# MLP of a two-layer trunk: down groups run in turns with up tiles, with seven products instead of eight for 5 of 8 pairs

## The chip, the cores and the metric

The kernel runs on one core of one Trainium2 chip. The core has five engines that run side by side, each through its own queue of instructions in a fixed order: TensorE (PE: matmuls out of SBUF into PSUM), VectorE (DVE) and ScalarE (ACT) for elementwise work, GpSimd (POOL) for elementwise work that touches SBUF alone, and SyncE (SP), which issues the loads here. Engines wait for each other by semaphores. The metric is the device time of one execution in microseconds (us); the runs of one kernel are given by their median.

## The reference

The trunk has two layers over 256 tokens of 2048 features (float32). Each layer is an attention part (a banded one in the first layer, a stick-breaking one in the second, both beside a memory attention), an output projection, and a squared-ReLU MLP. The change concerns the MLP:

```python
def rms_norm(x, g):
    xf = x.astype(jnp.float32)
    y = xf * lax.rsqrt(jnp.mean(xf * xf, axis=-1, keepdims=True) + EPS)
    return (y * g.astype(jnp.float32)).astype(x.dtype)

def sq_relu_mlp(h, g, w_in, w_out):
    return jnp.square(jax.nn.relu(rms_norm(h, g) @ w_in)) @ w_out
    # h (256, 2048), w_in (2048, 8192), w_out (8192, 2048)
```

Both products are wanted at close to float32 precision.

## The kernel before, in words

**Precision.** Every weight and every activation is split in two: `hi` is the value rounded to the fast matmul type (fp32r), `lo` is what is left of it. A product is then three matmuls, hi·hi, hi·lo and lo·hi. ScalarE makes `hi` (a cast, L173, L227, L249), VectorE makes `lo` (a subtraction, L176, L228, L250). Nearly all of VectorE's work is this.

**Weights.** They come as a stream of units of 128x1024 floats, in the order in which TensorE uses them. `weights()` hands out the next unit and keeps three more prepared ahead (`AHEAD = 3`); preparing one is the load, the cast and the subtraction. The pools hold 6 raw units, 4 `hi` and 5 `lo`, so no engine can run further ahead of TensorE than that.

**The MLP** goes through the 8192 hidden features in four chunks of 2048 (c = 0 to 3), 16 tiles of 128 features each. An *up tile* (f = 0 to 15) multiplies the normed input by 16 blocks of w_in: 16 matmuls 512 wide with `hi` weights (against both halves of the activation at once) and 16 matmuls 256 wide with `lo` weights. Its sum leaves PSUM by a copy on ScalarE (`low`) and an addition on VectorE. The norm's factor, which is one number per token, is applied behind the product: before the change `up` squares relu(x) on VectorE (L1138), and `finish` multiplies by the reciprocal of the mean square (`r_mlp`, made once in a layer by `inverse_square`: one matmul `inv`, L552, and a reciprocal on VectorE, L553) on VectorE (L1093), casts on ScalarE (L1094), and subtracts on GpSimd (L1095). Up tiles run in twos (`two_tiles`).

**Down groups.** After the 16 up tiles of a chunk come its down groups. A group is 1024 output features; two groups of four (g = 0 and 1 together, g = 2 and 3 together) make one `pair_group`, n = 0 or 1, which runs over the chunk's eight pairs j of feature tiles (2j, 2j+1). For one pair there are two ways. *Direct*: two units of weights, each 4 products, 8 in all, 24 matmuls 512 wide. *Sevenfold*: the 2x2 block form with seven products (Winograd's form of Strassen's), 21 matmuls 512 wide in four units of weights; its weight sums are made on VectorE (L222 to L226), and its sums of activations too (L1111), with their splits (L1124, L1125). The table `SEVEN` says which pairs are sevenfold: 25 in the first layer and 26 in the second, of 56 in each. A group's eight accumulators take all eight banks of PSUM, so up tiles and groups cannot be mixed. In the last chunk the second half of the outputs is done plainly (`tokens_major`, and by features at the very end).

**Order.** TensorE's instructions stand in program order. Those of the other engines are put in an order by a scheduler when the program is built, and stay in it.

## Time and profile before

| what | value |
|---|---|
| time, median of 3 runs | 2166.73 us (2166.26 to 2167.32) |
| span of the profiled execution | 2165.4 us, 1.3 us under that median |
| TensorE busy | 2158.2 us (100%) |
| VectorE busy | 1690.1 us (78%) |
| ScalarE busy | 1191.3 us (55%) |
| GpSimd busy | 326.7 us (15%) |
| read from HBM | 410.58 MB, 191 GB/s |
| first MLP | from about 440 us to 1130 us |
| second MLP | from about 1475 us to the end |

The span runs from the first to the last instruction of one execution. Busy is the time in which an engine had an instruction under way. Matmuls overlap: the recorded duration of one (389 ns for 512 columns) is longer than the distance at which the next one starts, and the distance is what counts.

### The profile page before, as it was taken

To read this page: it belongs to the slowest core of one execution; us is meant where nothing else is said; L and a number is where in the kernel's file an instruction comes from. 1 tells how busy PE (TensorE), PEld (TensorE's weight loads), DVE (VectorE), ACT (ScalarE), POOL (GpSimd) and SP (SyncE) were. 2 spreads that over 40 slices of the span, in tenths; PEclk is the share of its full clock that TensorE was granted. 3 is DMA by queue.
4 is the path that set the end of the run, shared out by engine and by line. 5 is a ranking of instruction groups with operands and counts; after the bars stand their busy time and mean duration, and the time that the engine had idled before them with its cause. 6 is when DMAs were issued, how large, how long until landed. Compare 5 with 4: busy or idle time off the path is not lost.

```text
span 2165.4 us, 30280 instructions
## 1 busy us (share of the span) xinstructions
PE 2158.2 (100%) x11083; PEld 1852.1 (86%) x11083; DVE 1690.1 (78%) x2431; ACT 1191.3 (55%) x1668; POOL 326.7 (15%) x349
## 2 busy tenths in 40 slices
PE   9999999999999999999999999999999999999999
PEld 8888888888888888888888889888888888988887
DVE  7778885678977987997886556567797798799796
ACT  7744545555655555555555447655565556555553
POOL 0010112621001001001050112352100100100100
PEclk9999999999999999999999999999999999999999
DMA  9655556655765765666666654455676577667665
GB/s 325 197 165 185 168 179 195 198 192 166 212 205 178 208 213 178 194 219 189 202 180 191 185 190 136 131 188 183 182 201 224 164 203 223 188 180 219 190 180 156
DMA packets 213317, 414.66 MB, mean 191 GB/s; under 512 B 13232, under 2 KB 144304, under 8 KB 213168
## 3 DMA queue, kind: packets, MB, share of 16 engines
q1 hardware_dynamic: 212592, 410.63, 62.0%
q8 instruction: 87, 1.43, 0.3%
q10 hardware_dynamic: 576, 2.10, 0.3%
q14 instruction: 62, 0.51, 0.1%
HBM read 410.58 MB, written 2.10 MB: 191 GB/s over the span
## 4 chain that ended last, share of the span: by engine, by line
PE 98%; DVE 1%; DMA 0%; issue 0%; ACT 0%; SPq 0%
PE acc L77 94%; PE yp L77 1%; PE accs L77 1%; PE tp L77 1%; PE s L77 1%; PE z L77 1%; DMA raw<-in_w_mem 0%; DVE lo L176 0%; DVE pt L640 0%; DVE lo L250 0%; DVE h L998 0%; ACT hi L173 0%; DVE kvx L465 0%; ACT hi L249 0%; PE stat L77 0%
## 5 line engine op out<-in xcount | busy, mean ns | idle before, releaser
L176 DVE TENSOR_TENSOR lo<-raw,hi 128x1024 fp32r<-128x1024 f32 (+1 forms) x524 | 642.6, 1237 | 308.4 <-ACT hi L173 183.3
L173 ACT CAST hi<-raw 128x1024 fp32r<-128x1024 f32 (+1 forms) x524 | 546.4, 1045 | 375.8 <-PE acc L77 316.7
L77 PE MATMUL acc<-hi,hid 128*128 128x512 f32 x1474 | 481.4, 389 | 0.0
L77 PE MATMUL acc<-mlpx,hi 128*128 128x512 f32 x2048 | 472.6, 390 | 0.0
L77 PEld LDWEIGHTS acc<-mlpx,hi 128*128 128x128 f32 x2048 | 382.0, 188 | 77.7
L77 PEld LDWEIGHTS acc<-hi,hid 128*128 128x128 f32 x1474 | 276.7, 188 | 57.5
L77 PE MATMUL acc<-lo,hid 128*128 128x512 f32 x737 | 286.7, 389 | 0.0
L1095 POOL TENSOR_TENSOR hid<-upsq,hid 128x256 fp32r<-128x256 f32 x128 | 122.3, 964 | 1086.2 <-ACT hid L1094 1086.2
L227 ACT CAST hi<-raw 128x1024 fp32r<-128x1024 f32 x204 | 192.1, 946 | 132.8 <-PE acc L77 56.0
L77 PEld LDWEIGHTS acc<-mlpx,lo 128*128 128x128 f32 x2048 | 250.6, 192 | 2.8
L77 PE MATMUL acc<-mlpx,lo 128*128 128x256 f32 x2048 | 252.0, 283 | 0.0
L228 DVE TENSOR_TENSOR lo<-raw,hi 128x1024 fp32r<-128x1024 f32 x204 | 222.8, 1108 | 29.6 <-ACT hi L227 28.0
L249 ACT CAST hi<-raw 128x1024 fp32r<-128x1024 f32 x146 | 154.0, 1055 | 126.1 <-PE acc L77 104.5
L77 PE MATMUL acc<-hi,xg 128*128 128x512 f32 x640 | 208.4, 398 | 0.0
L250 DVE TENSOR_TENSOR lo<-raw,hi 128x1024 fp32r<-128x1024 f32 x146 | 179.2, 1228 | 14.4 <-ACT hi L249 13.7
L77 PEld LDWEIGHTS acc<-lo,hid 128*128 128x128 f32 x737 | 138.4, 188 | 28.5
L77 PEld LDWEIGHTS acc<-hi,xg 128*128 128x128 f32 x640 | 120.2, 188 | 24.6
L451 ACT COPY low<-acc 128x256 f32<-128x256 f32 x188 | 69.1, 368 | 112.2 <-PE acc L77 111.9
L77 PE MATMUL acc<-lo,xg 128*128 128x512 f32 x320 | 124.7, 390 | 0.7 <-DVE lo L176 0.7
L77 PE MATMUL acc<-y,hi 128*128 128x512 f32 x512 | 119.9, 391 | 0.0
L77 PEld LDWEIGHTS acc<-y,hi 128*128 128x128 f32 x512 | 95.0, 188 | 19.0
L1094 ACT CAST hid<-upsq 128x256 fp32r<-128x256 f32 x128 | 51.9, 407 | 75.6 <-DVE upsq L1093 75.4
(202 smaller groups left out, 2610.4 us busy)
## 6 DMA issues: line engine op xcount, KB each, us to landing
raw<-in_w_up SPq DMA_DIRECT2D x256, 512.0 KB, 4.4
raw<-in_w_down SPq DMA_DIRECT2D x256, 512.0 KB, 5.6
raw<-in_w_in SPq DMA_DIRECT2D x80, 512.0 KB, 3.7
raw<-in_w_o SPq DMA_DIRECT2D x64, 512.0 KB, 4.0
raw<-in_w_mem SPq DMA_DIRECT2D x28, 512.0 KB, 5.9
raw<-in_w_kv_v SPq DMA_DIRECT2D x24, 512.0 KB, 3.9
raw<-in_w_kv_k SPq DMA_DIRECT2D x24, 512.0 KB, 4.2
raw<-in_w_q SPq DMA_DIRECT2D x24, 512.0 KB, 4.1
```

What stands on the lines that cost most here:

```text
L77: return self._tc.keep_in_program_order(fn(*args, **kwargs))
L173: nc.scalar.copy(hi[:, :n], raw[:, :n])
L176: nc.vector.tensor_tensor(lo, raw, hi.bitcast(F32), op=ALU.subtract)
L227: nc.scalar.copy(hi4, src)
L228: nc.vector.tensor_tensor(lo4, src, hi4.bitcast(F32), op=ALU.subtract)
L249: nc.scalar.copy(hi4, turned)
L250: nc.vector.tensor_tensor(lo4, turned, hi4.bitcast(F32), op=ALU.subtract)
L451: nc.scalar.copy(low[:], bank[:, T:])
L1094: nc.scalar.copy(hid[:, f, :T], a[:])
L1095: nc.gpsimd.tensor_tensor(hid[:, f, T:], a[:], hid[:, f, :T].bitcast(F32), op=ALU.subtract)
```

## The change

The change reorders the MLP and raises the number of sevenfold pairs.

- `SEVEN = [5, 5]`: in each of the 14 group pairs (seven in a layer), pairs j = 0 to 4 are sevenfold and j = 5 to 7 direct. That is 70 sevenfold pairs, where there were 51.
- `weave` gives each group eight up tiles to run in turns with: n = 0 gets the own chunk's tiles 8 to 15, n = 1 the next chunk's tiles 0 to 7. A group starts with one up tile, one sevenfold pair, one up tile, and so on (with direct units between them where n = 1). The activations of a layer live in one `hid` tile, whose features are overwritten as the group before them is through with them. The first chunk of each layer starts with its tiles 0 to 7 in `halves_first` and `two_tiles`, as before.
- PSUM: the accumulator "22" shares two banks with "p1" and "p5", which leaves a fourth bank in the pool that up tiles use.
- `inverse_square` is replaced by `inverse_root`: the mean square (VectorE, L576) is raised to the power -0.5 by a GpSimd instruction on 128x256 elements (L577). The factor `ri` is now applied ahead of the square: `finish` does max(x, 0) * ri on VectorE (L1168) and the square on ScalarE (L1171). The subtraction of the split moves from GpSimd to VectorE (`split`, L1126 and L1127).
- `block_sums` makes the sums of activations of a sevenfold pair (L1149 to L1152), one set for both groups.

Core of the diff:

```diff
-SEVEN = [
-    [(FOUR, FOUR), (THREE, FOUR), (THREE, FOUR), (THREE,)],
-    [(FOUR, FOUR), (THREE, FOUR), (THREE, FOUR), (FOUR,)],
-]
+SEVEN = [5, 5]
+BY_TURNS = 8
...
-    def inverse_square(acc, name):
+    def inverse_root(acc, name):
 
         ps = ps_y.tile([P, 512], F32, name="inv", tag="y")
         mm(ps[:, :T], neg_ones[:], acc[:], True, True)
-        r2 = const.tile([P, T], F32, name=f"r2_{name}", tag="r2")
-        nc.vector.tensor_scalar(r2[:], ps[:, :T], -1.0 / D, EPS, op0=ALU.mult, op1=ALU.add)
-        nc.vector.reciprocal(r2[:], r2[:])
-        return r2
+        ri = const.tile([P, T], F32, name=f"ri_{name}", tag="ri")
+        nc.vector.tensor_scalar(ri[:], ps[:, :T], -1.0 / D, EPS, op0=ALU.mult, op1=ALU.add)
+        nc.gpsimd.tensor_tensor(
+            ri[:], ri[:], neg_half[:, 0:1].to_broadcast([P, T]), op=ALU.pow
+        )
+        return ri
...
+        def split(hi, lo, src):
+            nc.scalar.copy(hi, src)
+            nc.vector.tensor_tensor(lo, src, hi.bitcast(F32), op=ALU.subtract)
+
+        def block_sums(c, j, a, b):
...
+            nc.vector.tensor_tensor(s23[:, P:], a11, a21, op=ALU.subtract)
+            nc.vector.tensor_tensor(s1, a21, a22, op=ALU.add)
+            nc.vector.tensor_tensor(s23[:, :P], s1, a11, op=ALU.subtract)
+            nc.vector.tensor_tensor(s14[:, P:], a12, s23[:, :P], op=ALU.subtract)
+            for home in homes[1:] if whole else homes:
+                split(*home)
...
-            def finish(f, hid=hid, squares=squares, factors=factors, c=c):
-                a = squares[f]
-                nc.vector.tensor_tensor(a[:], a[:], inv["r2"][:], op=ALU.mult)
-                nc.scalar.copy(hid[:, f, :T], a[:])
-                nc.gpsimd.tensor_tensor(
-                    hid[:, f, T:], a[:], hid[:, f, :T].bitcast(F32), op=ALU.subtract
+        def finish(c, f):
+            squares, factors = chunks[c]
+            a = squares[f]
+            nc.vector.scalar_tensor_tensor(
+                out=a[:], in0=a[:], scalar=0.0, in1=inv["ri"][:], op0=ALU.max, op1=ALU.mult
+            )
+            nc.scalar.activation(a[:], a[:], AF.Square)
+            if f // 2 >= sevens:
+                split(hid[:, f, :T], hid[:, f, T:], a[:])
+            elif f % 2 == 1:
+                split(hid[:, f, :T], hid[:, f, T:], a[:])
+                factors[f // 2] = block_sums(c, f // 2, squares.pop(f - 1), a)
...
+        for c, n, kind, i in mlp_steps(l):
+            if kind == "H":
+                halves_first(xg_, FIRST_UP, lambda f, b: up(0, f, b))
+                continue
+            if kind == "T":
+                two_tiles(xg_, [lambda b, f=f: up(0, f, b) for f in (i, i + 1)])
+                continue
+            if kind == "U":
+                features_major(xg_, lambda b, c=c, i=i: up(c, i, b))
+                continue
```

Three places in the order of the built programs matter below.

GpSimd at the start of the first layer's MLP, before (`sq` and `mlpsq` are the sums of squares that the norm needs, `upsq` a squared up tile, `kvsq` belongs to what follows the MLP):

```order
L963 TENSOR_TENSOR low_4145<-low,h_3211 128x256
L483 TENSOR_TENSOR sq<-h_3211 128x256
L484 TENSOR_TENSOR mlpsq_3214<-mlpsq_3214,sq 128x256
L1095 TENSOR_TENSOR hid_0_4160<-upsq,hid_0_4160 128x256 x16
L1095 TENSOR_TENSOR hid_1_5756<-upsq,hid_1_5756 128x256 x16
```

and with the change:

```order
L988 TENSOR_TENSOR low_4145<-low,h_3211 128x256
L507 TENSOR_TENSOR sq<-h_3211 128x256
L508 TENSOR_TENSOR mlpsq_3214<-mlpsq_3214,sq 128x256
L577 TENSOR_TENSOR ri_mlp_4279<-ri_mlp_4279,neg_half 128x256
L504 TENSOR_TENSOR kvsq<-h_3205 128x256
```

The subtractions of a layer (16 for each of four chunks) are gone from GpSimd, and one power instruction has come.

VectorE in the same place, before (`inv` is the sum over features in PSUM):

```order
L552 TENSOR_SCALAR r_mlp_4283<-inv 128x256
L553 RECIPROCAL r_mlp_4283<-r_mlp_4283 128x256
L1093 TENSOR_TENSOR upsq<-upsq,r_mlp_4283 128x256 x2
L176 TENSOR_TENSOR lo_4312<-raw_4310,hi_4311 128x1024
L176 TENSOR_TENSOR lo_4326<-raw_4324,hi_4325 128x1024
L1132 TENSOR_TENSOR up<-acc,low 128x256
```

and with the change, from 20 rows behind L576 on, at the end of the weights of the first sevenfold pair:

```order
L250 TENSOR_TENSOR raw_0_4596<-raw_0_4596 128x4x128
L252 TENSOR_TENSOR lo_4678<-raw_1_4598,hi_4677 128x1024
L252 TENSOR_TENSOR lo_4684<-raw_0_4596,hi_4683 128x1024
L1168 SCALAR_TENSOR_TENSOR up<-up,ri_mlp_4279 128x256 x6
L1149 TENSOR_TENSOR s_4466<-up 128x128
L1127 TENSOR_TENSOR hid_4160<-up,hid_4160 128x256
L1150 TENSOR_TENSOR up<-up 128x128
L1151 TENSOR_TENSOR s_4466<-up 128x128
L1127 TENSOR_TENSOR hid_4160<-up,hid_4160 128x256
```

The first use of the norm's factor stood directly behind its making; now it stands behind the last weights that can be prepared ahead, and all later weights stand behind it.

TensorE, with the change, from the end of up tile 8 into the first sevenfold pair of the first group (`mlpx` is the MLP's input, `hid` its activations, `s_x` and `s_w` sums of activations):

```order
L101 MATMUL acc<-mlpx_3213,lo_4546 128x256 x8
L101 MATMUL acc<-mlpx_3213,lo_4560 128x256 x8
L101 MATMUL acc<-hi_4600,hid_4160 128x512
L101 MATMUL acc<-lo_4601,hid_4160 128x512
L101 MATMUL acc<-hi_4600,hid_4160 128x512 x2
L101 MATMUL acc<-lo_4601,hid_4160 128x512
L101 MATMUL acc<-hi_4600,hid_4160 128x512
L101 MATMUL acc<-hi_4612,s_x 128x512
```

where before the other up tiles of the chunk stood (here tiles 8 and 9):

```order
L77 MATMUL acc<-mlpx_3213,lo_4555 128x256 x8
L77 MATMUL acc<-mlpx_3213,lo_4569 128x256 x8
L77 MATMUL acc<-mlpx_3213,lo_4595 128x256 x8
L77 MATMUL acc<-mlpx_3213,lo_4609 128x256 x8
L77 MATMUL acc<-mlpx_3213,lo_4658 128x256 x8
```

The first matmul that reads finished activations has moved forward by seven up tiles.

399 lines of the change are left out of this document (208 added, 191 removed).

## The prediction

> **What bounds the kernel now.** I read the page first, then the chain of waits, then a table of stretches, then the instructions around the start of an MLP.
>
> ```profile
> span 2165.4 us, 30280 instructions
> PE 2158.2 (100%) x11083; PEld 1852.1 (86%) x11083; DVE 1690.1 (78%) x2431; ACT 1191.3 (55%) x1668; POOL 326.7 (15%) x349
> PE 98%; DVE 1%; DMA 0%; issue 0%; ACT 0%; SPq 0%
> 449.37 643.53 PE acc L77 x3297
> 1484.29 521.83 PE acc L77 x2670
> 449.00:777.00 328.00, 328.00 (x1666) 281.11 (x1665) 276.11 (x373) 187.57 (x249) 30.18 (x32) 1.00 0.65 194
> 777.00:1093.00 316.00, 316.00 (x1637) 272.09 (x1636) 263.50 (x360) 170.10 (x225) 30.86 (x32) 1.00 0.65 199
> sum 1290.00, PE 1290.00 PEld 1107.92 DVE 1087.83 ACT 721.22 POOL 122.25; mean PE 322.50 PEld 276.98 DVE 271.96 ACT 180.31 POOL 30.56
> ```
>
> Line 3 is the share of each engine in the chain that ended last; lines 4 and 5 are two of its pieces (start, length, what). TensorE is never left waiting for 644 us in the first MLP and 522 us in the second. The table of stretches (width, then busy time of PE, PEld, DVE, ACT, POOL; its sum is over the two MLPs, 1290 us) has TensorE busy in all of it and VectorE in 1087.83 of 1290 us, 84%. So a matmul less is time less, as long as VectorE, which makes every `lo`, keeps ahead.
>
> The price of a matmul is the distance to the next one:
>
> ```profile
> 451.11 14.70 PE L77 MATMUL acc<-mlpx,hi 128*128 128x512 f32 x64
> 465.64 7.83 PE L77 MATMUL acc<-mlpx,lo 128*128 128x256 f32 x64
> 473.31 14.70 PE L77 MATMUL acc<-mlpx,hi 128*128 128x512 f32 x64
> ```
>
> 64 matmuls of 512 columns take 465.64 - 451.11 = 14.53 us, 0.227 each; 64 of 256 columns take 7.67 us, 0.120 each. An up tile (16 and 16) is 5.55 us, a sevenfold pair (21 wide) 4.77 us, a direct unit (12 wide) 2.72 us.
>
> **The change part by part.** *Products.* 70 - 51 = 19 pairs go from 8 products to 7, each product 3 matmuls: 57 wide matmuls less, 57 x 0.227 = **12.9 us less**. Switching between wide and narrow matmuls costs nothing visible at 465.64 and 473.31, so the new order costs TensorE nothing of its own.
>
> *VectorE in the mixed groups.* Its price is again the distance between starts:
>
> ```profile
> 530.26 0.41 DVE L1138 SCALAR_TENSOR_TENSOR upsq<-up 128x256 f32<-128x256 f32 x1
> 530.60 1.21 DVE L228 TENSOR_TENSOR lo<-raw,hi 128x1024 fp32r<-128x1024 f32 x1
> 531.73 0.42 DVE L1093 TENSOR_TENSOR upsq<-upsq,r_mlp 128x256 f32<-128x256 f32 x1
> 543.54 0.69 DVE L222 TENSOR_TENSOR raw<-raw 128x512 f32<-128x512 f32 x1
> 544.27 0.69 DVE L223 TENSOR_TENSOR raw<-raw,raw 128x512 f32<-128x512 f32 x1
> 546.48 0.68 DVE L225 TENSOR_TENSOR raw<-raw,raw 128x512 f32<-128x512 f32 x1
> 547.08 1.22 DVE L228 TENSOR_TENSOR lo<-raw,hi 128x1024 fp32r<-128x1024 f32 x1
> L1111 DVE TENSOR_TENSOR s<-upsq x62: 277/720/823, 472.5 to 2066.1; 128x128 f32<-128x128 f32 x62
> L1111 DVE TENSOR_TENSOR s<-s,upsq x31: 277/279/283, 474.3 to 2066.8; 128x128 f32<-128x128 f32 x31
> ```
>
> A 256-wide operation holds VectorE 0.34 us, a 1024-wide 1.13, a 512-wide 0.60 (0.73 when the next needs its result; 0.65 on average), a 128-wide 0.28. The first L1111 form has a median of 720 ns where 277 is possible; it is the one that starts while GpSimd subtracts (L1095), and the change takes those subtractions off GpSimd, so I count 0.28. Up tile: 2 x 1.13 + 3 x 0.34 = 3.28 (the subtraction that moves here replaces the multiplication that is merged away). Sevenfold pair: 4 x 0.65 + 3 x 1.13 + 0.60 = 6.6. Sums for one pair, beyond the splits counted: 4 x 0.28 + 0.34 + 0.28 = 1.74. A whole n = 1 group with its eight up tiles: 8 x 3.28 + 5 x 6.6 + 6 x 1.13 + 4 x 1.74 + 9 evacuations at 0.60 = 78.4 us, against 8 x 5.55 + 5 x 4.77 + 6 x 2.72 = 84.6 us of TensorE: 93%. An n = 0 group makes sums for one pair: 73.2 against 84.6. On the whole VectorE fits. Inside a group it is tight: two turns without a direct unit (tiles 3 and 4 of an n = 1 group) are 2 x 9.88 + 1.74 = 21.5 us against 20.6, so 0.9 us is lost in each of the six n = 1 groups if nothing is prepared ahead (5.4 us), nothing if the usual three units are. I take **2 us**. ScalarE gets 128 squares and has room (721 of 1290 us busy).
>
> *The power on GpSimd.* This is the term that decides. The factor was made by a reciprocal on VectorE at 449.86 and used at 451.65:
>
> ```profile
> 448.93 0.43 PE inv L77 x2
> 449.40 0.42 DVE L552 TENSOR_SCALAR r_mlp<-inv 128x256 f32<-128x256 f32 x1 [0.20 <-PE inv L77]
> 449.86 1.75 DVE L553 RECIPROCAL r_mlp<-r_mlp 128x256 f32<-128x256 f32 x1
> 451.65 0.76 DVE L1093 TENSOR_TENSOR upsq<-upsq,r_mlp 128x256 f32<-128x256 f32 x2
> ```
>
> Now GpSimd raises 256 columns to the power -0.5. No row shows that size. The nearest:
>
> ```profile
> L571 POOL TENSOR_TENSOR sroot<-msq,neg_half x20: 1007/1012/1983, 59.5 to 1221.1; 128x4 f32<-128x4 f32 x20
> L483 POOL TENSOR_TENSOR sq<-h x45: 610/796/1592, 366.8 to 1475.3; 128x256 f32<-128x256 f32 x45
> L720 POOL TENSOR_SCALAR_AFFINE_SELECT sp<-sp x12: 407/408/409, 1298.1 to 1384.2; 128x256 f32<-128x256 f32 x12
> L155 POOL TENSOR_SCALAR_AFFINE_SELECT neg_tri<-neg_ones 128x128 f32<-128x128 f32 x1 | 0.3, 293 | 0.0
> ```
>
> (minimum/median/maximum ns in the first three.) The same power takes 1007 ns for only **4** columns, where a multiplication of 256 takes 610: the power is dear by the column. How much of the 1007 is fixed? The select takes 293 ns for 128 columns and 408 for 256, so 0.9 ns a column and 178 fixed. A multiplication reads two operands and cannot be cheaper by the column, so at most 610 - 256 x 0.9 = 380 ns of it is fixed. Then the power costs between (1007 - 380)/4 = 157 and (1007 - 178)/4 = 207 ns a column, and 256 columns **40.6 to 53.2 us**. I take 42, near the end that comes from the same kind of instruction. (Were the 1007 ns all fixed, it would be about 1 us: the first rival.)
>
> What hides it: TensorE's work from 449.4 to the first use of finished activations. In the new order that is the rest of tiles 2 and 3, tiles 4 to 7 and tile 8: 112 wide and 96 narrow matmuls in all. That is to 473.31 by the rows above, then 32 wide (7.26) and tile 8 (5.55): 486.1 us. The power starts at about 449.9 and ends at 491.9. Behind it VectorE has six scalings, then the splits and sums in its order; up to the split of feature tile 0 that is 12 operations of 256 and 8 of 128, 12 x 0.34 + 8 x 0.28 = 6.3 us, and the first matmul needs only ScalarE's half of that split, some 0.5 us sooner: 5.8. So the first sevenfold pair starts at 497.7 and not at 486.1: **11.6 us lost**.
>
> Then VectorE is late, because everything queued behind the first scaling waited with it: all later weights, the evacuations of tiles 6 to 8, the splits of eight tiles, the sums of four pairs. From the end of the power to the last `lo` of the third sevenfold pair its order holds 10 of 1024 (11.3), 2 of 512 (1.2), 8 weight sums (5.2), 31 of 256 (10.5) and 25 of 128 (7.0): 35.2 us. TensorE needs that unit 3 x 4.77 + 2 x 5.55 - 1.36 = 24.0 us behind its restart, so at 5.8 + 24.0 = 29.8: **5.4 us more** (0 if ScalarE and VectorE overlap better than I add up). Further on a turn is 9.88 of VectorE against 10.3 of TensorE, so the lag does not grow. ScalarE's squares stand behind the same wait, with the casts of later weights behind them; they are the shorter queue.
>
> Per layer 11.6 + 5.4 = 17.0; two layers **34.0 us**. Sum: -12.9 + 34.0 + 2 = +23.1 on a span of 2165.4: 2188.5, and with the 1.3 us by which the median lies over it, 2189.8. I say **2190**.
>
> The Trainium skill speaks of the power's engine: "GPSIMD Engine Reference", section "Performance versus the Vector engine", has about 2.6 cycles per element for ordinary elementwise work there (4497 ns for an addition of 2048 columns). By that rule 256 columns would be an estimated 0.6 us (an eighth of it), which agrees with the row of 610 ns for a multiplication and not with 1007 ns for 4 columns of a power; by it the power would be hidden and the sum be -12.9 + 2.
>
> **The rivals.** *A, the power is cheap* (its 1007 ns are a fixed cost). It hides whenever it takes under 486.1 - 5.8 - 449.9 = 30.4 us; the whole change breaks even where a layer's loss is about 6 us, near 31 us. For it: no row shows that the cost grows with columns. Against it: 1007 ns is 2.5 times the largest fixed cost that the other GpSimd rows allow (380). Time: 2166.7 - 12.9 = 2154, **faster**.
> *B, the power at its upper end*, 53.2 us: 11.2 more in each layer, 2190 + 22 = 2212. For it: the fixed cost of the one operation measured at two sizes (178 ns).
> *C, VectorE becomes the bound in all mixed groups*: if operations cost their recorded duration (1.22 for 1024, 0.42 for 256) because each waits for ScalarE's cast, a turn is 3.7 + 7.1 = 10.8 us against 10.3; five turns in 14 groups, 70 x 0.5 = 35 us on top: 2225. For it: 93% load and only three units ahead. Against it: TensorE did not wait at all in the old groups, which held four sevenfold pairs with two direct units each (6.6 + 2 x 1.13 = 8.9 of VectorE against 10.2).
> *D, the lag is milder*: the wait is there, but nothing is lost behind it and in the groups: 2166.7 - 12.9 + 2 x 11.6 = 2177, and 2174 with the power at 40.6.
>
> **How the numbers follow.** Forecast (2180 to 2200) 0.55, D 0.13, B 0.14, C 0.07, A 0.08, something else 0.03. A measurement of this kernel tells about 0.2% (4.3 us) from no change. Only A is faster; a power of 30 to 33 us would end within 0.2%, which I give 0.03. So faster 0.08, same 0.03, slower 0.89. The range leaves out A, most of C and the end of B: 2172 to 2214.
>
> **What would show it.** Right: one GpSimd instruction L577 of some 42 us at the start of each MLP; a hole in TensorE of about 12 us behind up tile 8, near 486 and as far behind `inv` in the second layer, with L1168 released by L577 in the waits of VectorE; short holes in the second and third sevenfold pairs; no holes from the fifth pair on; 57 matmuls fewer; L1149 to L1152 near 0.28 us. Wrong: L577 of a few us (then A), holes in every turn (then C), or holes at the tiles that share one PSUM bank, 13 to 15 of a chunk, of which I expect none, since a direct unit of 2.72 us stands between them, in which VectorE's part of the evacuation is 0.34 us.

## The result: 2227 us, slower by more than predicted

| kernel | median of its runs | ratio to the kernel before, 95% interval |
|---|---|---|
| before | 2166.75 us (2166.26 to 2167.32) | |
| with the change | 2227.16 us (2225.93 to 2228.55) | 1.0279 (1.0265 to 1.0294) |

The change makes the kernel 60 us slower. I had predicted 2190, with 2214 as the upper end: the direction is right, the size is not. The page of the changed kernel, its parts 1 and 4:

```profile
span 2225.6 us, 30260 instructions
PE 2168.3 (97%) x11026; PEld 1842.7 (83%) x11026; DVE 1745.2 (78%) x2597; ACT 1246.7 (56%) x1828; POOL 285.5 (13%) x223
PE 87%; DVE 6%; POOL 4%; ACT 1%; issue 1%; DMA 0%; SPq 0%; ACTq 0%; DVEq 0%
```

TensorE has 57 matmuls less (11083 before), as the change says. Without waits this would be a span of 2165.4 - 12.9 = 2152.5 us; the span is 2225.6, so 73 us are lost. The chain of waits was 98% TensorE before and is 87% now, with GpSimd in it for the first time. The groups of instructions tell what TensorE's MLP matmuls waited for (busy time, mean ns of one, then idle time ahead of them and what ended it; before the change all these matmuls had 0.0, as in the first row here, which is of the kernel before), and the row of the power stands below them:

```profile
L77 PE MATMUL acc<-mlpx,hi 128*128 128x512 f32 x2048 | 472.6, 390 | 0.0
```

```profile
L101 PE MATMUL acc<-mlpx,hi 128*128 128x512 f32 x2048 | 490.5, 393 | 8.9 <-DVE up L1186 8.9
L101 PE MATMUL acc<-hi,hid 128*128 128x512 f32 x1404 | 476.3, 392 | 20.1 <-ACT hid L1126 20.1
L101 PE MATMUL acc<-lo,hid 128*128 128x512 f32 x702 | 276.5, 394 | 7.9 <-DVE lo L252 7.9
L101 PE MATMUL acc<-hi,s_w 128*128 128x512 f32 x280 | 99.5, 393 | 1.5 <-ACT hi L251 1.5
L101 PE MATMUL acc<-lo,s_w 128*128 128x512 f32 x140 | 56.8, 406 | 6.9 <-DVE lo L252 6.8
L101 PE MATMUL acc<-lo,s_x 128*128 128x512 f32 x80 | 31.7, 396 | 3.8 <-DVE lo L252 3.8
L577 POOL TENSOR_TENSOR ri_mlp<-ri_mlp,neg_half 128x256 f32<-128x256 f32 x2 | 82.3, 41140 | 14.3 <-DVE ri_mlp L576 14.3
```

That is 20.1 us for finished activations (the two holes behind the power), 8.9 us for an up tile's PSUM bank, and 20.1 us in four rows for the weights' `hi` and `lo`. Together 49.1 us. (The sum is smaller than 73, since a wait counts as idle only once the recorded 0.39 us of the matmul ahead are over, 0.16 us more than its distance to the next, and since part of the loss is a slower clock, 8.8 us, and some 9 us lie in distances that are a little longer, each by too little to count as idle.)

**The start of an MLP.** The chain of waits there, in order of time (start, length, what):

```profile
449.60 41.15 POOL ri_mlp L577
...
490.77 2.10 DVE up L1168 x6
...
505.96 0.34 DVE up L1186
...
506.44 13.73 PE acc L101 x54
```

and TensorE's own timeline (the bracket is the idle time ahead and what ended it):

```profile
483.92 2.07 PE L101 MATMUL acc<-mlpx,lo 128*128 128x256 f32 x16
496.06 0.80 PE L101 MATMUL acc<-hi,hid 128*128 128x512 f32 x1 [10.07 <-ACT hid L1126]
496.66 0.63 PE L101 MATMUL acc<-lo,hid 128*128 128x512 f32 x1
497.08 1.05 PE L101 MATMUL acc<-hi,hid 128*128 128x512 f32 x2
...
506.44 6.76 PE L101 MATMUL acc<-mlpx,hi 128*128 128x512 f32 x16 [3.98 <-DVE up L1186]
```

```profile
485.00:497.00 12.00, 1.93 (x11) 1.58 (x10) 8.34 (x24) 5.73 (x17) 5.74 (x1) 0.65 0.28 88
497.00:535.00 38.00, 33.32 (x144) 27.14 (x143) 33.35 (x62) 21.40 (x39) 0.00 (x0) 0.88 0.43 126
```

The power takes 41.15 us; the first sevenfold pair starts at 496.06 behind a hole of 10.07. Then a second hole: up tile 9 needs a bank whose evacuation (L1186, at 505.96) stands in VectorE's queue behind the splits of eight tiles. Behind each hole the granted clock is low (0.65 and 0.88 on the mean in the two stretches, the number ahead of the DMA share): 0.42 us from one wide matmul to the next instead of 0.23, and 6.76 us for 16 of them where 3.79 is usual. The Trainium skill, "TensorE: Matmul & The Clock Gate", section "Part 1: The HAM clock gate", says that the clock is halved behind an idle window of about 3.4 us and comes back after as long of work; the holes of 10.07 and 3.98 us agree. The clock is back after 2.9 and 6.1 us of matmuls (at 498.93 and 512.58). Run e1, below, has half clock behind a hole of only 1.94 us, which that sentence would not lead one to expect.

**The later groups.** (A turn, in what follows, is one up tile and one sevenfold pair, 10.3 us of TensorE.) One wait of a pattern that comes back in every layer and chunk, on the chain of waits around 871 us (third sevenfold pair of an n = 0 group):

```profile
871.39 0.38 ACT low L475
...
871.80 0.42 DVE up L1186
872.23 0.60 DVE raw L249
872.82 0.34 DVE up L1168
873.16 0.96 DVE lo L252
...
874.21 0.69 DVE raw L250
...
874.93 1.06 ACT hi L251
...
876.01 1.24 DVE lo L252
```

TensorE waits for `lo` at 874.1, for `hi` at 876 and for `lo` again at 877.2. The weight sums (L249, L250) and the subtractions of this pair come late in VectorE's queue. Measured by the distances of the matmuls' starts, such waits sum to some 15 us in each layer, mostly 2.3 to 3.4 us in an n = 0 group and 1.1 to 1.3 in an n = 1 group.

### The profile page after: what moved, and what is told of

Same layout as the page of the kernel before. It is cut to its first block, busy times and chain, and to the rows that moved or that the text cites. A ratio compares the mean times of both kernels' runs of the same rounds, so it can differ in the third digit from the quotient of the medians.

```text
span 2225.6 us, 30260 instructions
## 1 busy us (share of the span) xinstructions
PE 2168.3 (97%) x11026; PEld 1842.7 (83%) x11026; DVE 1745.2 (78%) x2597; ACT 1246.7 (56%) x1828; POOL 285.5 (13%) x223
## 4 chain that ended last, share of the span: by engine, by line
PE 87%; DVE 6%; POOL 4%; ACT 1%; issue 1%; DMA 0%; SPq 0%; ACTq 0%; DVEq 0%
PE acc L101 83%; POOL ri_mlp L577 4%; DVE lo L252 2%; PE yp L101 1%; PE accs L101 1%; PE tp L101 1%; PE s L101 1%; PE z L101 1%; ACT hi L251 0%; DVE raw L250 0%; DVE up L1168 0%; ACT hi L197 0%; DVE raw L249 0%; DVE up L1186 0%; DVE hid L1127 0%
## 5 line engine op out<-in xcount | busy, mean ns | idle before, releaser
L200 DVE TENSOR_TENSOR lo<-raw,hi 128x1024 fp32r<-128x1024 f32 (+1 forms) x524 | 640.3, 1236 | 243.1 <-ACT hi L197 211.1
L197 ACT CAST hi<-raw 128x1024 fp32r<-128x1024 f32 (+1 forms) x524 | 540.9, 1044 | 357.4 <-PE acc L101 293.1
L101 PE MATMUL acc<-mlpx,hi 128*128 128x512 f32 x2048 | 490.5, 393 | 8.9 <-DVE up L1186 8.9
L101 PE MATMUL acc<-hi,hid 128*128 128x512 f32 x1404 | 476.3, 392 | 20.1 <-ACT hid L1126 20.1
L251 ACT CAST hi<-raw 128x1024 fp32r<-128x1024 f32 (+1 forms) x280 | 263.8, 944 | 221.1 <-DVE raw L247 147.6
L252 DVE TENSOR_TENSOR lo<-raw,hi 128x1024 fp32r<-128x1024 f32 (+1 forms) x280 | 302.3, 1086 | 41.1 <-ACT hi L251 36.4
L101 PEld LDWEIGHTS acc<-hi,hid 128*128 128x128 f32 x1404 | 265.0, 189 | 73.3 <-ACT hid L1126 20.6
L101 PE MATMUL acc<-lo,hid 128*128 128x512 f32 x702 | 276.5, 394 | 7.9 <-DVE lo L252 7.9
L101 PEld LDWEIGHTS acc<-mlpx,lo 128*128 128x128 f32 x2048 | 261.1, 191 | 9.5 <-DVE lo L200 0.3
L101 PE MATMUL acc<-mlpx,lo 128*128 128x256 f32 x2048 | 265.0, 283 | 0.0
L274 DVE TENSOR_TENSOR lo<-raw,hi 128x1024 fp32r<-128x1024 f32 x108 | 133.2, 1233 | 46.6 <-ACT hi L273 46.5
L273 ACT CAST hi<-raw 128x1024 fp32r<-128x1024 f32 x108 | 113.9, 1054 | 84.7 <-PE acc L101 65.6
L101 PE MATMUL acc<-hi,s_w 128*128 128x512 f32 x280 | 99.5, 393 | 1.5 <-ACT hi L251 1.5
```

The lines of the kernel that those rows point to most:

```text
L101: return self._tc.keep_in_program_order(fn(*args, **kwargs))
L197: nc.scalar.copy(hi[:, :n], raw[:, :n])
L200: nc.vector.tensor_tensor(lo, raw, hi.bitcast(F32), op=ALU.subtract)
L251: nc.scalar.copy(hi4, src)
L252: nc.vector.tensor_tensor(lo4, src, hi4.bitcast(F32), op=ALU.subtract)
L273: nc.scalar.copy(hi4, turned)
```

## Experiments on the power

All ratios below are to the kernel before, run beside them (2166.3 to 2166.9 us in every set). Line numbers move a little from kernel to kernel. "Idle" is the sum of the rows above in the groups view, 49.1 us in the changed kernel; with any idle time ahead of the MLP's other matmuls (3.5 us in e2, at most 2.7 in the others).

| run | median us | ratio (95% interval) | idle |
|---|---|---|---|
| e1_lnexp | 2199.01 | 1.0148 (1.0133 to 1.0163) | 25.2 |
| e2_power_alone (in the kernel before) | 2173.32 | 1.0031 (1.0019 to 1.0042) | 3.5 |
| e3_lnexp_early | 2197.91 | 1.0147 (1.0130 to 1.0163) | 25.1 |
| e4_warm | 2228.19 | 1.0284 (1.0264 to 1.0305) | 31.1 |

**e1: the change without GpSimd's power.** The factor is made by two functions of ScalarE.

```diff
-        nc.gpsimd.tensor_tensor(
-            ri[:], ri[:], neg_half[:, 0:1].to_broadcast([P, T]), op=ALU.pow
-        )
+        nc.scalar.activation(ri[:], ri[:], AF.Ln)
+        nc.scalar.activation(ri[:], ri[:], AF.Exp, scale=-0.5)
```

> The changed kernel with the norm's factor made by two ScalarE operations (Ln, then Exp of -0.5 times it) instead of the power on GpSimd; all else is the same. In the profile of the changed kernel TensorE loses 72.7 us in the two MLPs against its own pace: 42 in the stretch from the power to the second sevenfold pair behind it (waits of 10.2 in each layer, 4.1 and 5.1 at the next up tile, 4.4 in each at half clock, 1.8 in each later), 31 in single waits spread over the later groups. Theory P (the two parts are separate): the 42 go, the 31 stay: 2185. Rival Q (the later waits are lateness carried on from the power): they go too, below 2162.

28 us come back, not 42 and not all 60. Without the power the first group still loses 6.7 us in the first layer (its fourth step waits 0.95 us, up tile 9 2.1 us for its bank, 1.6 us go to the half clock and the rest to waits in its next pairs) and some 5 us in the second: VectorE makes the sums of four pairs just there. And the later waits, but for small ones near the end of a layer, are the same to a hundredth. So the loss has two halves: the power, 28 us, and 45 us in the mixed order itself.

The second layer loses less because its clock stays up: behind the same hole of 1.94 us the 16 wide matmuls of tile 9 take 5.48 us in the first layer and 3.91 in the second. In e1 half clock appears once more, in the second layer's last chunk (from 2064.7 us, for 6.8 us), behind waits of 1.54, 0.25 and 0.53 us. These two stretches cost 1.6 and 2.8 us, and the executions of one kernel differ in how many they have.

**e2: the power in the kernel before.** The reciprocal on VectorE becomes a power of -1 on GpSimd.

```diff
-        nc.vector.reciprocal(r2[:], r2[:])
+        nc.gpsimd.tensor_tensor(
+            r2[:], r2[:], neg_ones[:, 0:1].to_broadcast([P, T]), op=ALU.pow
+        )
```

> The kernel before with the reciprocal on VectorE replaced by a power of -1 on GpSimd, on the same 128x256 elements, and nothing else. Theory P (41 us matter only because finished activations are wanted 37 us behind the power's start): here they are wanted 16 up tiles later, some 78 us, so 2167 to 2172. Rival (a long GpSimd instruction costs in itself, by holding what VectorE shares with it, or by the queue behind it): 2180 or more.

6.7 us, also with 41.14 us for each power; that is 1.3 us over the 2172 that I had as upper end. Where finished activations are wanted only behind all sixteen up tiles, the same instruction is nearly hidden: what costs is the early use, with everything queued behind it. (What is left is that queue again: behind the power VectorE does nine scalings in a row, and near 515 and 518 us TensorE waits 0.46 and 1.09 us for a `lo`.) The rival, that a long instruction on GpSimd slows VectorE, finds nothing in the trace: beside the power of the changed kernel VectorE's 1024-wide subtractions still take 1.22 us.

**e4: the hole filled.** 45 matmuls whose result nobody reads go ahead of the first sevenfold pair.

```diff
+            if (c, n, i) == (0, 0, 0) and kind == "S":
+                warm = ps_y.tile([P, 512], F32, name="warm", tag="y")
+                for _ in range(45):
+                    mm(warm[:], xg_[:, 0, :P], xg_[:, 0, :], True, True)
```

> The changed kernel with 45 idle matmuls of 512 columns (10.2 us, into a bank that is free there) between up tile 8 and the first sevenfold pair, which fill the hole in which TensorE waits for the power. If the half clock behind the hole is a cost of its own: 1.4 to 4.4 us less in each layer, 2218 to 2224. If VectorE is late there anyway, the next up tile waits as much longer: 2226 to 2229.

```profile
485.77 10.39 PE L101 MATMUL warm<-mlpx 128*128 128x512 f32 x45
506.32 5.87 PE L101 MATMUL acc<-mlpx,hi 128*128 128x512 f32 x16 [5.01 <-DVE up L1186]
```

Up tile 9 starts at 506.32 instead of 506.44. The clock stays up in the first pair, and the wait for the bank grows by about as much (5.01 against 3.98). So in this stretch the half clock costs nothing by itself: VectorE's queue sets when tile 9 can start. Behind it the first layer is 1.1 us ahead of the changed kernel (third pair's wait ends at 527.4 and not 528.5), which does not reach the total: the profiled execution has half clock in the first layer's last chunk (from 1029.3 us, for 6.8 us), where that of the changed kernel has none.

## Experiments on the waits in the mixed groups

| run | median us | ratio (95% interval) | idle |
|---|---|---|---|
| e5_pinned | 2198.3 | 1.0146 (1.0131 to 1.0161) | 26.4 |
| e6_spaced | 2224.38 | 1.0265 (1.0250 to 1.0281) | 38.1 |
| e7_spaced_power | 2248.23 | 1.0380 (1.0363 to 1.0397) | 53.9 |
| e8_sums_on_scalar | 2195.22 | 1.0131 (1.0111 to 1.0152) | 23.9 |
| e9_direct_later | 2192.98 | 1.0121 (1.0106 to 1.0136) | 21.8 |
| e10_no_sums_of_pair_4 | 2184.32 | 1.0085 (1.0068 to 1.0102) | 16.4 |
| e11_ten_tiles_early | 2188.42 | 1.0101 (1.0086 to 1.0116) | 16.6 |
| e12_ten_tiles_power | 2210.3 | 1.0202 (1.0182 to 1.0223) | 32.5 |

**e3 and e5: is it VectorE's order?** My first theory (O) was that VectorE evacuates a tile, for which it stands idle 0.79 us, ahead of the next pair's weights. In e3 the next units are prepared between the two halves of an up tile:

```diff
             if i == 1:
                 slot()
+                while len(prepared) < AHEAD + 1 and state["next"] < len(stream):
+                    prepare()
```

> As the run with Ln and Exp, and each up tile prepares the next units of weights (up to the same three ahead) between its two halves, so ahead of its own evacuation and not behind it. Theory O (the 31 us come from the order: the weights of the third and fourth unit of a sevenfold pair stand behind the evacuation of the up tile, for which VectorE waits): at least 20 of the 31 us go, 2155 to 2165. Theory T (VectorE has too much work in the mixed groups): nothing goes, 2181 to 2189.

The waits stayed, but the run proves nothing: the scheduler put VectorE's rows back into nearly the order of e1. In e5 the evacuation is pinned as well:

```diff
-            nc.vector.tensor_tensor(t[:], bank[:, :T], low[:], op=ALU.add)
+            pin(nc.vector.tensor_tensor(t[:], bank[:, :T], low[:], op=ALU.add), not early)
```

> As e3_lnexp_early (factor by two ScalarE functions, the next units prepared between the two halves of an up tile), and in addition VectorE's addition that evacuates an up tile is pinned behind the last weight subtraction traced before it, so that the sums and the lo of the next sevenfold pair really stand ahead of the tile in VectorE's order. Theory O (order: VectorE stands for ScalarE's copy of a tile, 0.79 us, with the sums of the next pair queued behind it): the waits of 0.86 + 0.42 + 1.03 us in the third sevenfold pair of an n = 0 group and of 1.08 in the n = 1 groups go, some 13 us per layer; 2170 to 2180, unless the later evacuation makes up tiles wait for their bank. Theory W (work: VectorE has more to do in the first three turns of a group, with the evacuations of the group before and the block sums in it, than its look-ahead of three units covers): the time stays within 2190 to 2202, the waits move by a few instructions but their sum in a group stays.

Here the order did change, and the time did not: 2198.3. The waits moved by a few instructions and to the next turns. Theory O falls.

**e8: is it the additions of finished banks?** Theory W said that VectorE carries work over from the end of the group before.

```diff
-                    if self.c == 0 and q not in ("11", "p6"):
+                    if q not in ("11", "p6"):
                         nc.scalar.copy(dst, src)
```

> As e1_lnexp, but at a group's end only the banks 11 and p6 are added by VectorE; the other sums are plain copies by ScalarE in every chunk, as the changed kernel does in the first chunk (this leaves the accumulation over chunks out for them). It takes 6 or 7 additions of 0.6 us off VectorE, about 4 us, at the end of each group from the second chunk on. Theory W: the waits of 2.6 us in n = 0 groups of chunks 1 and 2 and of 1.3 us in n = 1 groups go or fall below 0.5, the 3.4 us of the last chunk falls too: about 16 us less in both layers than e1, 2180 to 2186. Theory O: the waits stay, 2195 to 2200.

Some 4 us came back where 13 to 19 were expected. The waits of the n = 0 groups of chunks 1 and 2 stayed at 2.6 us to a hundredth, although VectorE now had 2.1 us of idle time in the 11 us ahead of the turn before it. So it is not work carried over from far: each wait belongs to its own turn. Theory W falls in this form.

**e6 and e7: an order of mine that was at fault.** (In the orders, U is an up tile, S a sevenfold pair, A and B are the two direct units of a pair.)

> As e1_lnexp, and each group runs its first two up tiles one behind the other, and direct units between later sevenfold pairs: n = 0: U8 U9 S0 U10 S1 U11 S2 A5 U12 S3 U13 S4 U14 A6 U15 B5 B6 A7 B7, n = 1: U0 U1 S0 A5 U2 S1 A6 U3 S2 U4 S3 A7 U5 S4 U6 B5 U7 B6 B7. The same instructions in another order. Each group gives VectorE one tile's slack (5.55 - 3.28 = 2.3 us) ahead of its first sevenfold pair. Theory W: the 2.6 us waits of n = 0 fall to about 0.3, the 3.4 us of the last chunk to about 1, the 1.1 to 1.3 us of n = 1 go, and the first group's 6.7 us per layer fall to 0 to 2: 2198 - 32 to 40 = 2158 to 2166. Theory O: every pair that follows an up tile is as late as before, only the first group gains: 2180 to 2192.

> The order of e6_spaced with GpSimd's power kept (41.1 us). The first sevenfold pair stands one up tile later, 5.55 us. If the price of the power (28 us in e1 against the changed kernel) is that finished activations are wanted before it ends, 5.55 of the 10.2 us hole are filled in each layer and the half clock behind it is shorter: e6 + 10 to 18 us. If the price came from VectorE's queue behind the power alone, whatever TensorE does meanwhile: e6 + 24 to 28 us.

```profile
L81 PE MATMUL acc<-hi,hid 128*128 128x512 f32 x1404 | 485.2, 399 | 31.1 <-ACT hid L1105 23.0 <-DVE hid L1106 7.8
```

In the n = 1 groups I put up tile 1 of the next chunk ahead of the first sevenfold pair. Its splits overwrite the features which that pair still has to read: the pair multiplies features of the next chunk, and it waits for them to be made, 3.3 us in such a group and 1.7 in the last one of each layer. In the n = 0 groups A5, only one sevenfold pair behind tile 11, waits 0.8 and 0.9 to 1.1 us for that tile's splits. These two mistakes cover what the runs were for; they say nothing on O and W. One thing can be read: e7 less e6 is 24 us, so an up tile more ahead of the first pair saves only 4 of the power's 28 in this order (why, is seen in e12).

**e9 and e10: is it the block sums?** Going through the list of waits again, I saw that each falls in the turn into which `block_sums` of a pair of tiles falls (behind tile 9 where n = 0, behind tiles 1 and 3 where n = 1), if that turn holds no direct unit. This is theory B: such a turn asks 12.0 us of VectorE, by the prices of its operations, against 10.3 of TensorE. Its rival L says that turns without a direct unit run dry, sums or not. e9 moves one step:

```diff
-n = 1: U0 S0 A5 U1 S1 A6 U2 S2 A7 U3 S3 U4 S4 U5 ...
+n = 1: U0 S0 A5 U1 S1 A6 U2 S2 U3 S3 A7 U4 S4 U5 ...
```

> As e1_lnexp (2198.3 to 2199), with one step moved: in n = 1 groups the direct unit A7 stands behind the fourth sevenfold pair instead of the third (U0 S0 A5 U1 S1 A6 U2 S2 U3 S3 A7 U4 S4 ...). Theory B (block sums): a wait arises in the sevenfold pair in whose turn the block sums of a pair of tiles fall (behind tiles 1 and 3 in n = 1, behind tile 9 in n = 0) and no direct unit: such a turn asks 9.88 + 1.74 + 0.34 = 12.0 us of VectorE against 10.3 of TensorE, and the look-ahead cannot carry it. Then the n = 1 waits of 1.08 + 1.33 + 1.33 us per layer go, nothing comes in their place at the fourth pair (its turn has no sums), 7 us less: 2190 to 2193. Theory L (every run of turns without a direct unit runs dry, sums or not): the wait moves to the fourth or stays at the fifth pair: 2196 to 2200.

6 us less, as theory B has it: the 1.33 us waits of chunks 1 and 2 are gone, nothing came at the fourth pair (in chunk 0, 0.7 of 1.1 us stayed).

```diff
+                if f // 2 == 4:
+                    split(hid[:, 8, :T], hid[:, 8, T:], squares.pop(8))
+                    factors[4] = [
+                        [hid[:, t, k + m * P : k + (m + 1) * P] for k in (0, T)]
+                        for t, m in ((8, 0), (8, 1), (9, 0), (9, 1), (8, 0))
+                    ]
+                    return
                 factors[f // 2] = block_sums(c, f // 2, squares.pop(f - 1), a)
```

> As e1_lnexp, but for the pair of tiles 8 and 9 the four block sums and the splits of them are left out; plain blocks of the two tiles stand in their place (so the products of this pair are not those that are wanted). Nothing else changes. It takes 4 x 0.28 + 0.34 + 0.28 - 0.34 = 1.4 us of VectorE and the turns between ScalarE and VectorE out of each n = 0 group. Theory B: the waits in the third pair of n = 0 groups (2.6, 2.6 and in the last chunk 3.4 us) and the small ones behind them (0.3 to 0.7) go: 2 x 9 = 18 us less than e1: 2178 to 2184. Theory L: at most 1.4 us a group, 2190 to 2198, with waits left at the same place.

14.7 us less. With 1.4 us of VectorE taken out, the waits of 2.3 to 2.6 us in the third pair of chunks 1 and 2 are gone altogether, though five turns without a direct unit still follow each other: L falls. The waits of the n = 1 groups stay, and so does the last chunk's 3.4 us, which I had counted in. TensorE in the third pair of chunk 2, in e1 and then at the same step in e10:

```profile
859.85 0.50 PE L101 MATMUL acc<-lo,hid 128*128 128x512 f32 x1 [0.70 <-DVE lo L252]
...
862.78 0.50 PE L101 MATMUL acc<-lo,s_w 128*128 128x512 f32 x1 [0.76 <-DVE lo L252]
```

```profile
854.67 0.39 PE L101 MATMUL acc<-lo,hid 128*128 128x512 f32 x1
```

The profiled execution of e10 has no half clock in its MLPs, behind the same hole of 1.9 us at tile 9. That is not shown to be the edit's doing: it is also the shortest of the four (2181.6 us at a mean clock of 1.000; the others take 2183.3 to 2186.0 at 0.999 and 0.998). VectorE's timeline of e1 shows a turn with the sums:

```profile
852.80 0.29 DVE L1149 TENSOR_TENSOR up<-up 128x128 f32<-128x128 f32 x1
...
853.60 0.42 DVE L1126 TENSOR_TENSOR hid<-up,hid 128x256 fp32r<-128x256 f32 x1
853.94 0.29 DVE L1150 TENSOR_TENSOR s<-up 128x128 f32<-128x128 f32 x1
854.14 0.42 DVE L1126 TENSOR_TENSOR hid<-up,hid 128x256 fp32r<-128x256 f32 x1
854.48 0.69 DVE L246 TENSOR_TENSOR raw<-raw 128x512 f32<-128x512 f32 x1
855.08 0.29 DVE L1151 TENSOR_TENSOR s<-up,s 128x128 f32<-128x128 f32 x1
```

Sums of pair 4 (L1149 to L1151) and its splits (L1126) stand ahead of and among the weight sums (L246 is the first of four) of the pair that TensorE reaches at 856.7 and then waits for. In that pair's turn VectorE is itself idle twice, 0.79 us for ScalarE's copy `low` and 0.78 us for a `hi`. The runs do not tell the time of the sums from this to and fro between the two engines: leaving the sums out shortens both.

**e11 and e12: the sums moved.** Tiles 8 and 9 are made in the group before, beside direct units.

```diff
-n = 0: U8 S0 U9 S1 U10 S2 U11 S3 U12 S4 U13 A5 U14 A6 U15 B5 B6 A7 B7
-n = 1: U0 S0 A5 U1 S1 A6 U2 S2 A7 U3 S3 U4 S4 U5 U6 B5 U7 B6 B7
+n = 0: S0 U10 S1 U11 S2 U12 S3 U13 S4 A5 U14 A6 U15 B5 B6 A7 B7
+n = 1: U0 S0 A5 U1 S1 A6 U2 S2 U3 S3 A7 U4 S4 U5 U6 B5 U7 B6 U8 U9 B7
...
-range(FIRST_UP, BY_TURNS, 2)
+range(FIRST_UP, 10, 2)
```

> As e1_lnexp, with tiles 8 and 9 of a chunk made in the group before (in the first chunk: as one more pair of tiles at its start), so that their block sums fall beside direct units, and A7 as in e9: n = 0: S0 U10 S1 U11 S2 U12 S3 U13 S4 A5 U14 A6 U15 B5 B6 A7 B7, n = 1: U0 S0 A5 U1 S1 A6 U2 S2 U3 S3 A7 U4 S4 U5 U6 B5 U7 B6 U8 U9 B7. The same products, sums and splits. Theory B: the waits of all groups but the first go (18 + 7 us), and the first pair of a layer, 5.55 us later, has more time for its sums: of 6.7 us per layer 0 to 3 are left. 2199 - 25 - 8 to 13 = 2160 to 2166, against 2166.7 of the kernel before. Theory L: the turns of n = 0 still run dry: 2185 or more.

> The order of e11_ten_tiles_early with GpSimd's power of 41.1 us kept. TensorE reaches its first sevenfold pair 5.55 us later than in the changed kernel. If the price of the power is that finished activations are wanted before it ends, the first hole falls from 10.2 to about 4.6 us and the train behind it (4.1 to 5.1 us for a bank, 4.4 at half clock, 1.8 in later pairs) shrinks with it: e11 + 12 to 22 us. If VectorE's queue behind the power sets it alone: e11 + 24 to 28.

e11 came out 22 us above the upper end of what theory B promised, and L's "2185 or more" came true as a number. Its mechanism did not: the third to fifth pairs of the n = 0 groups of chunks 1 and 2, with no direct unit between them, do not wait. The first group did as expected (1.9 us left of 6.7), but the n = 0 group of chunk 2 now loses 2.2 us in its *first* pair (that of chunk 1 0.9 us in its second), and the last chunk loses 8.7 and 7.3 us in its first two (3.2 and 1.6 of that at half clock). VectorE and ScalarE ahead of that first pair, and TensorE in it:

```profile
831.65 0.69 DVE L232 TENSOR_TENSOR lo<-raw,hi 128x512 fp32r<-128x512 f32 x1 [3.13 <-ACT hi L231]
```

```profile
831.00 0.62 ACT L231 CAST hi<-raw 128x512 fp32r<-128x512 f32 x1 [2.02 <-PE acc L81]
```

```profile
839.76 0.49 PE L81 MATMUL acc<-hi,s_w 128*128 128x512 f32 x1 [0.51 <-ACT hi L231]
841.02 0.50 PE L81 MATMUL acc<-lo,s_w 128*128 128x512 f32 x1 [0.77 <-DVE lo L232]
```

VectorE stands idle for 3.13 us, waiting for a `hi` for which ScalarE waits on TensorE's matmuls, and ten microseconds later the weights are 2.2 us late. VectorE did not work ahead although it had nothing else to do. By the prices of the rows, it has 7.5 us from the first free `hi` of tile 9 to the fourth step of the pair, and that pair's weights, the tile's evacuation and the sums of pair 4 ask 10 (theory H, with the pools of buffers as what bounds the look-ahead).

In e12 the power costs 22 us in this order, the upper end of what I expected, and the first hole is 8.43 us, not the 4.6 that one tile more would leave. The trace shows why, on GpSimd and on VectorE:

```profile
449.88 41.14 POOL L557 TENSOR_TENSOR ri_mlp<-ri_mlp,neg_half 128x256 f32<-128x256 f32 x1 [7.13 <-DVE ri_mlp L556]
```

```profile
494.96 2.09 DVE L1148 SCALAR_TENSOR_TENSOR up<-up,ri_mlp 128x256 f32<-128x256 f32 x6
```

The power ends at 491.02, and the scalings that wait for it begin only at 494.96 (in the changed kernel at 490.77, as soon as the power ends). In VectorE's order the sums and `lo` of the first pair's weights stand ahead of them, and these began late, at 489.03, behind a wait of 4.14 us for TensorE. So 3.9 us of the hole are VectorE's order and the other 4.5 the power, as expected. In e7 the same two times are 490.59 and 493.71.

## The wait's cause, and a version that beats both kernels

| run | median us | ratio (95% interval) | idle |
|---|---|---|---|
| e13_ten_tiles_two_units | 2175.8 | 1.0040 (1.0027 to 1.0053) | 9.3 |
| e14_one_more_hi | 2230.25 | 1.0293 (1.0278 to 1.0308) | 46.6 |
| e15_both | 2212.01 | 1.0207 (1.0191 to 1.0222) | 34.4 |
| e16_adds_pinned | 2165.22 | 0.9992 (0.9983 to 1.0001) | 4.1 |
| e17_tile_first | 2163.45 | 0.9985 (0.9976 to 0.9994) | 3.7 |

```diff
-n = 1: ... U5 U6 B5 U7 B6 U8 U9 B7
+n = 1: ... U5 U6 B5 U7 U8 U9 B6 B7
```

> As e11, with two direct units instead of one between tile 9 and the first sevenfold pair of the next group (n = 1: U0 S0 A5 U1 S1 A6 U2 S2 U3 S3 A7 U4 S4 U5 U6 B5 U7 U8 U9 B6 B7), and in the last chunk the additions of the second column pair (six of 0.6 us) begin behind the fifth sevenfold pair instead of at the group's start. Theory H (the look-ahead is bound by the buffers of hi and lo, so a turn must hold its own sums: from the time that the first hi of tile 9 comes free to the fourth step of the pair, VectorE needs 10 us and e11 gives it 7.5): the 2.2 us at the first pair of the n = 0 groups go, those of the last chunk (4.3 + 3.9) fall to 2 or less, 15.8 per layer become about 5: 2188 - 2 x 10 = 2164 to 2172. Otherwise the waits move to other pairs and the time stays within 2182 to 2190.

One direct unit, 2.72 us, moved into the turn with the sums takes the 2.2 us waits away (0.5 is left) and the first pair's 4.3 us of the last chunk: 12.6 us less with no instruction less. That is theory H's step, somewhat smaller than I put it; it is slack in the turn with the sums, as B asks for, and does not show by itself that the buffers bound the look-ahead. What is left in the last chunk is its second pair, on VectorE and TensorE:

```profile
1005.96 0.68 DVE L1018 TENSOR_TENSOR d<-d,e 128x512 f32<-128x512 f32 x1
...
1008.29 0.69 DVE L1018 TENSOR_TENSOR e<-e,e 128x512 f32<-128x512 f32 x1
```

```profile
1018.23 0.49 PE L81 MATMUL acc<-hi,s_x 128*128 128x512 f32 x1 [1.19 <-ACT hi L231]
1019.89 0.50 PE L81 MATMUL acc<-lo,s_x 128*128 128x512 f32 x1 [1.17 <-DVE lo L232]
```

The additions of the column pairs (L1018, six of 0.6 us), which I had meant to move behind the fifth pair, had been put back by the scheduler. e14 and e15 change the buffers:

```diff
-    raws = ctx.enter_context(tc.tile_pool(name="raws", bufs=6))
-    his = ctx.enter_context(tc.tile_pool(name="his", bufs=4))
+    raws = ctx.enter_context(tc.tile_pool(name="raws", bufs=5))
+    his = ctx.enter_context(tc.tile_pool(name="his", bufs=5))
```

> As e1_lnexp, with five buffers for hi instead of four and, to make room, five for the loaded weights (raw) instead of six. Theory H: ScalarE can cast one unit earlier, the waits of 2.6 us in n = 0 groups lose one 1024-wide operation (1.1 us) each and those of 1.08 to 1.33 in n = 1 groups fall to 0.3 or less; about 6 to 10 us less over both layers, 2189 to 2193, unless a raw fewer makes loads late (then new waits on the DMA queue appear, and the time goes up). If the buffers are not what bounds the look-ahead: the waits stay as they are, 2197 to 2200.

> e13 and e14 together. If e14's extra buffer gains and no load is late: a few us below e13, 2158 to 2168. If loads are late it is slower than e13.

```profile
720.93 1.05 ACT L273 CAST hi<-raw 128x1024 fp32r<-128x1024 f32 x1 [2.11 <-DMA raw<-in_w_down]
```

Both are slower by some 31 and 36 us than their partners, with ScalarE waiting for loads, as the "unless" said: a raw buffer less is dearer than a `hi` more is worth. Whether the number of `hi` buffers alone bounds the look-ahead is therefore left open; there was no room to add one without taking another away.

e16 pins the six additions and moves A5:

```diff
-                nc.vector.tensor_tensor(dst, dst, src, op=ALU.add)
+                pin(nc.vector.tensor_tensor(dst, dst, src, op=ALU.add), n == 1)
...
-n = 0: S0 U10 S1 U11 S2 U12 S3 U13 S4 A5 U14 A6 ...
+n = 0: S0 U10 S1 U11 S2 U12 A5 S3 U13 S4 U14 A6 ...
```

> As e13, where the six additions of the second column pair in the last chunk did not move (VectorE still made them at 1006 to 1016 us, beside the 3.0 us wait of the second sevenfold pair). Here they are pinned behind the work traced before them and begin behind A6, and in n = 0 groups A5 stands behind U12 instead of behind the fifth pair (S0 U10 S1 U11 S2 U12 A5 S3 U13 S4 U14 A6 U15 B5 B6 A7 B7). If those 3.6 us of additions make the wait, 3.0 of the 10.9 us that e13 still loses per layer go and the 0.65 at the pair ahead of A5: 2 x 3.6 to 4.3 less: 2166 to 2170. If the waits come from the turn itself: 2172 to 2177.

e17 puts tile 10 ahead of the first sevenfold pair in the first chunk only:

```diff
+c = 0, n = 0: U10 S0 U11 S1 U12 S2 A5 S3 U13 S4 U14 A6 U15 B5 B6 A7 B7
```

> As e16, and only in the first chunk tile 10 stands ahead of the first sevenfold pair, not behind it (U10 S0 U11 S1 U12 S2 A5 S3 U13 S4 ...). In e16 the first two pairs of a layer lose 1.07 and 0.86 us, with the block sums of five pairs just ahead of them. If these sums are what is late, 5.55 us more let them finish: 2 x 1.5 to 1.9 less, 2161 to 2163, under the kernel before by some 0.2%. If VectorE's turn is what is late, the wait moves to S2 and S3, which now have a direct unit and no tile between them: 2164 to 2168.

10.6 us less in e16, somewhat more than the two moves were priced at, and 1.8 more in e17. Some 2 us of the 10.6 are the clock: e13 runs at a mean of 0.998 to 0.999 in four of five executions and takes 1.2 to 2.6 us longer there than at 1.000, and e16 is at 1.000 in all. The wait of the second pair in the last chunk is gone, and so is the 0.6 us at the pair ahead of A5; e16 made both moves at once, so that each wait goes by its own move is read from the place and not tested apart. e17 is 63.7 us faster than the changed kernel and 0.15% faster than the one before, with the same 70 sevenfold pairs. The page and the groups of e17 that had waits in the changed kernel:

```profile
span 2162.3 us, 30274 instructions
L83 PE MATMUL acc<-mlpx,hi 128*128 128x512 f32 x2048 | 483.3, 390 | 0.8 <-DVE up L1167 0.8
L83 PE MATMUL acc<-hi,hid 128*128 128x512 f32 x1404 | 471.3, 391 | 0.4 <-DVE d L1075 0.4
L83 PE MATMUL acc<-lo,hid 128*128 128x512 f32 x702 | 274.4, 391 | 1.4 <-DVE lo L234 1.4
L83 PE MATMUL acc<-lo,s_w 128*128 128x512 f32 x140 | 55.0, 392 | 0.8 <-DVE lo L234 0.8
```

Its span is 9.8 us over the 2152.5 that the products alone would give; 3.7 of them are such idle time (3.4 in these rows, 0.3 ahead of the narrow matmuls). By the distances of starts the waits are 5.4, and some 4 us more than in the kernel before lie in distances a little longer than usual; why is not shown, so that the new order costs TensorE nothing of its own, as I had it, is not shown either.

## Why the prediction was half right

The three terms by the spans: -12.9 for the products, +28.8 for the power (changed kernel less e1) and +44.3 for the mixed groups (e1 less 2152.5) make +60.2, where I had -12.9, +34 and +2.

*Products, 12.9 us less.* Right in its count: 57 matmuls fewer. The version with hardly a wait left comes within 9.8 us of that sum, so it has 3.1 of the 12.9 us to show.

*The power.* Its own time, 42 us, was right: 41.14. So was the hole, 11.6 against 10.07. With the 1007 ns for 4 columns that makes (41140 - 1007) / 252 = 159 ns a column, at the low end of the two bounds. The estimate of 0.6 us by the Trainium skill's "GPSIMD Engine Reference", section "Performance versus the Vector engine", comes near the multiplications and additions here (0.61 us at the least, 0.8 to 1.3 on the mean of a row) and not near this power, which takes some 70 times that estimate. The 5.4 us of lag was too small: behind the hole there came 4 to 5 us for tile 9's bank, 4.4 us at half clock and 1.8 us in the next pairs, some 20.5 and 21.4 us in the two layers against my 17.0. I had a bank wait down only for tiles 13 to 15, and no clock term. But e1 shows that 6.7 and 5 us of the loss there come without the power too, so taking it away brings 28 us, less than my 34.

*VectorE in the mixed groups, 2 us.* This is the step that failed. It measured about 31 us, and 5 to 6.7 more per layer in the first groups, 45 us in all (the span of e1, 2196.8, less 2152.5, is 44.3; 4.4 of it at half clock). The prices in it hold: 1.14 us from one 1024-wide operation to the next, 0.28 us for L1149 to L1152, 9.88 us for a turn. I even had the wait of an n = 1 group, 0.9 us against 1.1 to 1.3 measured, and then took most of it away, because "the usual three units are" prepared. And for n = 0 groups I divided VectorE's work by the time of the whole group, 73.2 of 84.6 us, and found room. But the sums of a pair all fall into one turn, which then asks 12.0 us of VectorE in 10.3, by the same prices, and work done ahead does not cover it: e10 without the sums has no wait there, and e13 with a direct unit more in the turn has next to none. In the last chunk the additions of the column pairs did the same (e16). Why VectorE cannot work further ahead is open: the number of buffers is argued, and e14, meant to show it, made loads late.

*The rivals.* C, VectorE as the bound in all mixed groups, had the nearest time, 2225, by luck and for another reason: by it each operation costs its recorded duration and every turn is late. The distances stayed at 0.34 and 1.14 us, and one or two turns in a group wait, not five. A (a cheap power) and B (53 us) fall with 41.14. D had the power's hole and nothing behind it, and falls with both.

*"No holes from the fifth pair on"* was wrong, by the same step.

## What to carry to other kernels

A mean load of 87 to 93% on a helper engine says nothing about waits, if its work comes in lumps and the look-ahead is short: add up the helper's work turn by turn, between the time at which a buffer comes free and the time at which its result is wanted, and put slack (here a unit that asks little of VectorE) into the turn with the lump. Before an operation is given to an idle engine, find its price at the real size, and count what is queued behind its first user. A wait that looks the same to a hundredth of a microsecond when work is taken off elsewhere belongs to its own turn.

## What the runs showed of the hardware

- GpSimd's power: 41.14 us for 128x256 in four places alike (two in the changed kernel, two in e2), an estimated 159 ns a column, beside 0.61 us at the least for a multiplication of the same size. VectorE's 1024-wide subtractions keep their 1.22 us beside it.
- The clock halves behind holes of 4 to 10 us, and stays there for some 3 to 6 us of matmuls (0.42 us from one wide matmul to the next, instead of 0.23). It also halved behind a hole of 1.94 us (e1, first layer, and not behind the same hole in the second) and behind waits of 0.51 and 1.25 us with one matmul between them (e11, near 1012 to 1014 us). Filling the hole kept the clock in the first pair and gained nothing in the total (e4): VectorE was late anyway, and half clock came later in another place.
- VectorE's 128-wide operations take 0.28 us once GpSimd no longer subtracts beside them (281 ns the median of L1149 in the changed kernel; before, 720 ns for the 56 of 62 that ran while GpSimd subtracted, and 279 ns for the other six).
